# RWKV products over four quarters of TensorE's array, with plain transposes between two layouts

## The chip, the core and the metric

The kernel runs on one core of one Trainium2 chip. Its time is device microseconds from start to end of one execution. The core's engines run their own instruction streams and wait for one another by semaphores: PE (TensorE, matrix products), DVE (VectorE), ACT (ScalarE), POOL (GpSimd), and SP, which in this kernel only issues DMAs. The profile keeps PE's weight loads apart from its products as PEld.

## The reference, cut to what matters

Two transformer blocks run one after the other on 256 tokens with 1024 features, in float32. Block 1 is differential attention and a mixture of 16 experts. Block 2 mixes a sparse attention and an RWKV-7 branch and then goes through a mixture of 32 experts. The change touches the RWKV branch alone, which has 8 heads of 64 features and is a recurrence over tokens:

```python
def step(state, inp):
    r_t, d_t, k_t, v_t, kk_t, b_t = inp
    sa = jnp.einsum('bhij,bhj->bhi', state, -kk_t)
    state = state * d_t[:, :, None, :] + sa[..., None] * b_t[:, :, None, :] + v_t[..., None] * k_t[:, :, None, :]
    y = jnp.einsum('bhij,bhj->bhi', state, r_t)
    return state, y
```

The experts' weights are 6 MB for each expert in either block and are read once.

## The kernel before

**Layout of the RWKV branch.** The 256 tokens are cut into 4 chunks of 64. Two heads lie on the two halves of the 128 partitions, so four pairs of heads times four chunks make 16 places, and a tile of 16 x 64 columns holds one 64 x 64 matrix for each of 8 heads and 4 chunks. `H2` is the pair of partition halves, `r_` one of them. Every product in `products` and `chunk_chain` is 64 x 64 by 64 x 64 (or 64 x 128), and it reads and writes the same half: `T.matmul(ps[r_, i], a[r_, i], b[r_, i])`. Two such products, one for each half, thus stand on two of the four quarters of the array, the ones on its diagonal.

**`products`** makes the triangular matrix of each chunk (`prod`, line 1646), masks it (line 1650) and inverts it in five levels (lines 1702 to 1732): `abT` by `X` (line 1707), a mask on DVE (line 1710), `Pm` by `XT` (line 1717), a subtraction on DVE (line 1721), and `XT` turned into the next `X` by products with the identity (line 1727) and a copy on ACT (line 1730). The generator `side` holds work that the levels do not need yet: `tokens` turns four tensors from features on partitions to tokens on partitions, by products with the identity too (line 1659), and a second `prod`. `take(side, 2)` inserts two of its steps at a time. **`chunk_chain`** applies the inverse (line 1753), makes the operators of a chunk (lines 1765 to 1774), their sums `N` (lines 1781 to 1785), two links of the recurrence (line 1792) and the output (lines 1803 to 1809). Everything takes its PSUM banks from one ring of four, `pr`.

**Order of the work.** There is no planner of times: `weave` draws steps from generators, always from the one whose summed yields are lowest, and while these run it hands steps of a `fill` generator in between. Of each positive yield a share of 0.4 is credit for the fill, and a step of the fill (`fm3g`, three products of 128 x 128 by 256 columns, lines 684 to 686) costs 0.33. The order so drawn is the order of instructions on each engine. Block 2 weaves four generators with this fill:

```python
weave((ds.topk(), 0.5),
      (chain(ds.qkv(x), ds.heads(lambda: bank(c))), 1.0),
      (conditions(), 0.8),
      (rwkv(), 1.0), fill=fill(), ratio=0.4, waits=0.1)
```

The fill holds the gates of both branches and the projection of the attention branch; what is left of it when the generators end is run behind them. `conditions` multiplies modulation weights on DVE (lines 460 to 463), and the weights of each projection are split into two parts by ACT and DVE (lines 628 and 629).

**SBUF units and the stream of weights.** SBUF is handed out in `NU` units of 8 KB per partition (1 MB each). `Stream` holds some of them as slots; it loads weights in a fixed order on SP's queue, and each load waits until its slot's last reader is done. Ahead of the experts of block 2 the stream takes 14 units (`st.size(14)`, line 2193), and `st.grow()` (lines 2220 and 2225) adds what is free. Each expert takes six loads of 1 MB.

Of the kernel before, what the change touches and what calls it, by code (L numbers as in the profile page):

```python
# [16 lines left out]
P = 128  # L17
# [5 lines left out]
NU = 21  # L23
# [1467 lines left out]

class Rwkv:
# [131 lines left out]
    def products(self, pb):  # L1624

        c, sl = self.c, self.sl
# [3 lines left out]
        abT, X, XT, Pm = (sl.get(64) for _ in range(4))  # L1630
# [22 lines left out]
        def tokens(src, dst, cp):  # L1653
# [23 lines left out]

        def others():
            yield from tokens(chunks(self.bt), bb[:, :, 0], A.copy)
            sl.free(self.bt)  # L1680
            vt, ktt = self.vt, self.ktt = chunks(self.v), chunks(self.kt)
            yield from tokens(vt, vt, A.copy)
            self.akT, self.bkT = sl.get(64), sl.get(64)
            yield from prod(self.kt, self.akT, self.bkT)
            yield from tokens(ktt, ktt, A.copy)
            self.uR = c.un.raw()
            self.R = two(self.uR)
            yield from tokens(kkr[:, :, 0], self.R[:, :, 1], A.copy)

            for o in os:  # L1690
# [7 lines left out]
                yield 1.1 / 2  # L1698
            sl.free(self.akT)
        side = others()  # L1700

        for l in range(1, 6):
            for o in os:
                ps = half()
                for i in range(8):
                    for r_ in H2:
                        T.matmul(ps[r_, i], abT[r_, o.start + i], X[r_, o.start + i], start=True, stop=True)
                    if i == 3:
                        yield 1.1 / 2
                V.tensor_tensor(Pm[:, o], ps, bc(c.lev[:, l], 8), ALU.mult)  # L1710
                yield 1.1 / 2
                yield from take(side, 2)
# [10 lines left out]
            for o in os if l < 5 else ():  # L1723
                px = half()
                for i in range(8):
                    for r_ in H2:
                        T.matmul(px[r_, i], XT[r_, o.start + i], c.ident[r_, r_], start=True, stop=True)
                    if i == 3:
                        yield 1.1 / 2
                A.copy(X[:, o], px)  # L1730
                yield 1.1 / 2
                yield from take(side, 2)
        yield from side
        sl.free(abT, X, Pm)

    def chunk_chain(self, pb):
# [23 lines left out]
        for hp in range(4):  # L1760
            ps = quarter()
            for ci in range(4):
                i = 4 * hp + ci
                for r_ in H2:
                    T.matmul(fl(ps[r_, ci]), UG[r_, i, 1], fl(bb[r_, i]), start=True, stop=True)
                if ci == 1:
                    yield 0.9 / 2
# [8 lines left out]
        for o in os:  # L1776
            ps = half()
            for i in range(8):
# [4 lines left out]
                if i == 3:  # L1783
                    yield 3.0 / 2
# [13 lines left out]
        for o in os:  # L1798
            ps = half()
            for i in range(8):  # L1800
# [6 lines left out]
                if i == 3:  # L1807
                    yield 3.9 / 2
# [605 lines left out]
```

## Time and profile before

| | us |
|---|---|
| median of 3 runs | 1343.98 (1343.59 to 1347.93) |
| the profiled execution, its own time | 1341.36 |
| its span, first to last instruction | 1339.8 |

| engine | busy us | share of the span |
|---|---|---|
| PE | 1146.8 | 86% |
| PEld | 705.4 | 53% |
| DVE | 592.5 | 44% |
| ACT | 347.0 | 26% |
| POOL | 101.7 | 8% |

The span is 1.6 us shorter than the execution's own time; a sum of changes inside the span carries over to that time. The shares are means over stages with different limits and have to be read by stage. A product of float32 matrices that is not a transpose is recorded as two instructions, so 320 recorded ones on line 1707 are 160 products.

### The profile page before, as it was taken

To read this page: it belongs to the slowest core of one execution; us is meant where nothing else is said; L and a number is where in the kernel's file an instruction comes from. 1 tells how busy PE (TensorE), PEld (TensorE's weight loads), DVE (VectorE), ACT (ScalarE), POOL (GpSimd) and SP (SyncE) were. 2 spreads that over 40 slices of the span, in tenths; PEclk is the share of its full clock that TensorE was granted. 3 is DMA by queue.
4 is the path that set the end of the run, shared out by engine and by line. 5 is a ranking of instruction groups with operands and counts; after the bars stand their busy time and mean duration, and the time that the engine had idled before them with its cause. 6 is when DMAs were issued, how large, how long until landed. Compare 5 with 4: busy or idle time off the path is not lost. (4 is left out here: it accounts for less than half of the span.)

```text
span 1339.8 us, 20574 instructions
## 1 busy us (share of the span) xinstructions
PE 1146.8 (86%) x8434; PEld 705.4 (53%) x8434; DVE 592.5 (44%) x1464; ACT 347.0 (26%) x675; POOL 101.7 (8%) x111
## 2 busy tenths in 40 slices
PE   5899977899998986988999999889876797677775
PEld 2777767444434335876788888844332242233221
DVE  4477653333225137698555747343222222222212
ACT  3335331211111124552232224232111111111111
POOL 2421110000001003002410010000000000000000
PEclk7999978899999996999999999989889988999898
DMA  8777756699996953350135628769999999999996
GB/s 302 288 276 267 277 223 274 282 418 419 420 384 246 418 218 123 127 187 34 64 140 208 205 94 331 281 256 417 420 419 420 419 420 420 419 420 418 421 419 267
DMA packets 60516, 404.09 MB, mean 302 GB/s; under 512 B 7328, under 2 KB 7584, under 8 KB 14464
## 3 DMA queue, kind: packets, MB, share of 16 engines
q1 hardware_dynamic: 58464, 400.58, 74.6%
q10 hardware_dynamic: 1824, 2.00, 0.5%
q8 instruction: 68, 1.11, 0.3%
q0 software_dynamic: 128, 0.13, 0.2%
q14 instruction: 32, 0.26, 0.1%
HBM read 401.64 MB, written 1.05 MB: 301 GB/s over the span
## 5 line engine op out<-in xcount | busy, mean ns | idle before, releaser
L1218 PE MATMUL a<-u,u 128*32 128x512 f32 (+1 forms) x1536 | 297.8, 614 | 36.2 <-DMA u<-in_expert_w_up 25.3
L1198 DVE SCALAR_TENSOR_TENSOR gs<-a,gc,gt 128x512 f32<-128x512 f32 (+1 forms) x50 | 37.5, 750 | 367.5 <-PE a L1227 360.2
L1227 PE MATMUL a<-u,hid 128*32 128x512 f32 (+1 forms) x736 | 135.5, 623 | 40.7 <-DMA u<-in_expert_w_down 40.7
L1218 PEld LDWEIGHTS a<-u,u 128*32 128x32 f32 (+1 forms) x1536 | 71.1, 119 | 176.6 <-issue 106.9
L684 PE MATMUL a<-u,u 128*128 128x256 f32 x656 | 141.5, 292 | 1.9 <-DVE u L629 1.9
L684 PE MATMUL a<-u,hi 128*128 128x256 f32 x640 | 136.5, 304 | 0.4 <-ACT u L1531 0.4
L1156 ACT COPY gs<-a 128x512 f32<-128x512 f32 x48 | 28.1, 586 | 335.8 <-PE a L1218 326.1
L684 PEld LDWEIGHTS a<-u,u 128*128 128x128 f32 x656 | 104.4, 193 | 12.7 <-issue 9.2
L684 PEld LDWEIGHTS a<-u,hi 128*128 128x128 f32 x640 | 99.3, 191 | 15.6 <-issue 8.9
L1200 ACT CAST u<-gs 64x512 fp32r<-64x512 f32 x96 | 59.2, 616 | 183.3 <-DVE gs L1198 182.2
L1227 PEld LDWEIGHTS a<-u,hid 128*32 128x32 f32 (+1 forms) x736 | 33.3, 119 | 124.2 <-DMA u<-in_expert_w_down 52.1
L1202 DVE TENSOR_TENSOR u<-gs,u 64x512 fp32r<-64x512 f32 x96 | 65.9, 686 | 27.2 <-ACT u L1200 25.3
L628 ACT CAST hi<-u 128x1024 fp32r<-128x1024 f32 x48 | 49.8, 1047 | 72.0 <-PE a L684 60.0
L629 DVE TENSOR_TENSOR u<-u,hi 128x1024 fp32r<-128x1024 f32 x48 | 61.7, 1291 | 14.7 <-ACT hi L628 14.2
L908 PE MATMUL a<-u,u 128*128 128x256 f32 x256 | 49.0, 312 | 9.2 <-DVE u L629 8.0
L629 POOL TENSOR_TENSOR u<-u,u 128x512 fp32r<-128x512 f32 (+1 forms) x22 | 44.5, 2041 | 127.2 <-ACT u L628 127.2
L1163 PEld LDWEIGHTS a<-sel,gs 128*128 128x128 f32 x256 | 35.1, 212 | 28.4 <-issue 26.3
L1254 PE MATMUL acc<-u,PT 128*128 128x512 f32 x128 | 44.4, 460 | 5.2 <-DVE u L1202 3.6
L1140 PE MATMUL a<-pm,u 128*128 128x256 f32 x256 | 40.8, 315 | 8.1 <-DVE gs L1198 3.2
L908 PEld LDWEIGHTS a<-u,u 128*128 128x128 f32 x256 | 40.4, 216 | 10.3 <-DVE u L629 8.2
L1254 PEld LDWEIGHTS acc<-u,PT 128*128 128x128 f32 x128 | 22.3, 208 | 44.1 <-DVE u L1202 34.3
L763 PE MATMUL e<-u,u 128*128 128x256 f32 x288 | 40.1, 306 | 5.5 <-ACT u L591 5.0
(447 smaller groups left out, 1599.9 us busy)
## 6 DMA issues: line engine op xcount, KB each, us to landing
u<-in_expert_w_gate SPq DMA_DIRECT2D x96, 1024.0 KB, 19.9
u<-in_expert_w_up SPq DMA_DIRECT2D x96, 1024.0 KB, 19.9
u<-in_expert_w_down SPq DMA_DIRECT2D x96, 1024.0 KB, 19.9
u<-in_ada_w SPq DMA_DIRECT2D x32, 1024.0 KB, 6.9
u<-in_w_in SPq DMA_DIRECT2D x19, 1024.0 KB, 4.9
u<-in_ada_w SPq DMA_DIRECT2D x32, 512.0 KB, 3.9
u<-in_attn_w_in SPq DMA_DIRECT2D x12, 512.0 KB, 7.8
u<-in_attn_w_in SPq DMA_DIRECT2D x6, 1024.0 KB, 7.4
```

The lines of the kernel that those rows point to most:

```text
L628: nc.scalar.copy(h[:, o], w[:, o])
L629: (nc.vector if e == "v" else nc.gpsimd).tensor_tensor(l[:, o], w[:, o], h[:, o].bitcast(F32), ALU.subtract)
L684: c.nc.tensor.matmul(ps, a[:, k, c0:c0 + n], b[:, k], start=k == 0 and i == 0, stop=k == kn - 1 and i == 2)
L763: T.matmul(p[:, j * S:(j + 1) * S], l, r, start=(h, j, k, n) == (0, 0, 0, 0), stop=(h, k, n) == (1, 3, 2), skip_group_check=True)
L908: self.c.nc.tensor.matmul(ps[:, j * S:(j + 1) * S], a[:, k, j * P:(j + 1) * P], b[:, k], start=k + j + i == 0, stop=k == KD - 1 and i == 2 ...
L1140: nc.tensor.matmul(ps[:, jj * m:(jj + 1) * m], h[:, t, k * P:(k + 1) * P], pm[:, t], start=i + jj + t == 0, stop=i + t == 2, skip_group_ch ...
L1198: c.nc.vector.scalar_tensor_tensor(out=y[o], in0=py[o], scalar=gc[o], in1=gt[o], op0=ALU.mult, op1=ALU.mult)
L1200: c.nc.scalar.copy(yy[H2[q], q], y[H2[q]])
L1202: c.nc.vector.tensor_tensor(yy[H2[1 - q], q], y[H2[q]], yy[H2[q], q].bitcast(F32), ALU.subtract)
L1218: c.nc.tensor.matmul(pg[r:r + cap], xe[:, k0 + k, x0:x0 + cap], w[:, k, :], start=k0 + k < nk, stop=k0 + k >= KD - nk)
L1227: c.nc.tensor.matmul(py[r:r + cap], hT[:, f], w[:, f - f0, q * 512:(q + 1) * 512], start=f < nk, stop=f >= 4 - nk)
L1254: c.nc.tensor.matmul(acc[:, 2 * t + q], PT[:, t * P:(t + 1) * P], yy[:, q], start=False, stop=stop, skip_group_check=True)
```

## The change

All quarters of the array get work. A second layout puts the tokens of a chunk on the half of the chunk's parity (even chunks on partitions 0 to 63, odd ones on 64 to 127), and features stay on the half of the head. A product that contracts over features and writes tokens (or the other way) then reads one half and writes either, and four products that follow each other, `quads(y)`, stand on four different quarters. This holds for `prod`, the first product of a level, the operators, the sums and most of the output; products from tokens to tokens stay on two quarters. The two row halves of a group of four write to two different PSUM banks. Going from one layout to the other is now a plain transpose of 128 x 128 (`turned`), where it was a product with a 64 x 64 identity. The first product of a level needs `abX`, the matrix in the other layout, which is made by 32 more products and two copies on ACT. The terms of the recurrence's output that come from the chunk before get a PSUM bank of their own and are added on DVE. A copy of `kkr` on ACT goes ahead of one turn. Yields and the numbers of side steps taken change with the steps. `NU` goes from 21 to 22, and the kernel is built with a smaller scratch area for dynamic DMAs.

```diff
-NU = 21
+NU = 22
...
+def quads(y):
+    return [(2 * y + c, h, 2 * y + h) for c in range(2) for h in range(2)]
...
         def prod(src, o1, o2):
             lhs = chunks(src)
-            for hp in range(4):
-                ps = pb()
-                p4 = ps.rearrange("p (c a s) -> p c a s", c=4, a=2)
-                for ci in range(4):
-                    i = 4 * hp + ci
-                    for r_ in H2:
-                        T.matmul(fl(p4[r_, ci]), lhs[r_, i], fl(kkr[r_, i]), start=True, stop=True)
-                    if ci == 1:
-                        yield 0.9 / 2
-                for o, a in ((o1, 0), (o2, 1)):
-                    V.tensor_tensor(o[:, 4 * hp:4 * hp + 4], p4[:, :, a], bc(c.mlt[:, a], 4), ALU.mult)
-                yield 0.9 / 2
...
+            for x in (0, 8):
+                ps = [pb().rearrange("p (c a s) -> p c a s", c=4, a=2) for _ in H2]
+                for y in range(4):
+                    for i, h, j in quads(x // 2 + y):
+                        T.matmul(fl(ps[h][H2[i % 2], y]), lhs[H2[h], i], fl(kkr[H2[h], i]), start=True, stop=True)
+                    yield 0.3
+                for h in range(2):
+                    for o, a in ((o1, 0), (o2, 1)):
+                        V.tensor_tensor(o[:, x + h:x + 8:2], ps[h][:, :, a], bc(c.mlt[:, a], 4), ALU.mult)
+
+        def turned(src, dst, cp):
             for o in os:
                 ps = half()
-                for i in range(8):
-                    for r_ in H2:
-                        T.matmul(ps[r_, i], src[r_, o.start + i], c.ident[r_, r_], start=True, stop=True)
-                    if i == 3:
-                        yield 1.1 / 2
+                for i in range(0, 8, 2):
+                    T.transpose(fl(ps[:, i:i + 2]), src[:, o.start + i:o.start + i + 2], c.ident)
+                    if i % 4:
+                        yield 0.3
                 cp(dst[:, o], ps)
-                yield 1.1 / 2
...
+        for o in os:
+            ps = half()
+            for i in range(8):
+                for r_ in H2:
+                    T.matmul(ps[r_, i], chunks(self.bt)[r_, o.start + i], kkr[r_, o.start + i, 0], start=True, stop=True)
+                if i == 3:
+                    yield 1.1 / 2
+            A.copy(abX[:, o], ps)
+            yield 1.1 / 2
+        sl.free(abT)
...
         for l in range(1, 6):
-            for o in os:
-                ps = half()
-                for i in range(8):
-                    for r_ in H2:
-                        T.matmul(ps[r_, i], abT[r_, o.start + i], X[r_, o.start + i], start=True, stop=True)
-                    if i == 3:
-                        yield 1.1 / 2
-                V.tensor_tensor(Pm[:, o], ps, bc(c.lev[:, l], 8), ALU.mult)
-                yield 1.1 / 2
-                yield from take(side, 2)
+            ps = half(), half()
+            for y in range(8):
+                for i, h, j in quads(y):
+                    T.matmul(ps[h][H2[i % 2], y], abX[H2[h], i], X[H2[h], i], start=True, stop=True)
+                if y % 2:
+                    yield 0.35
+            for h in range(2):
+                V.tensor_tensor(Pm[:, h::2], ps[h], bc(c.lev[:, l], 8), ALU.mult)
+            yield from take(side, 4)
...
+            if l < 5:
+                for _ in turned(XT, X, A.copy):
+                    yield 0.3
+                    yield from take(side, 1)
...
+        def two_sums(pairs):
+            ps = half(), half()
+            for z, (a, b) in enumerate(pairs):
+                for y in range(8):
+                    for i, h, j in quads(y):
+                        T.matmul(ps[i % 2][H2[h], y], a[H2[i % 2], j], b[H2[i % 2], j], start=z + y == 0, stop=z == 1,
+                                 skip_group_check=True)
+                    if y % 2:
+                        yield 0.4
+            return ps
+        ps = yield from two_sums([(ktt, vt), (bb[:, :, 0], UG[:, :, 0])])
+        for a in range(2):
+            A.copy(N[:, a::2], ps[a])
...
+        ps = yield from two_sums([(vt, self.bkT), (UG[:, :, 0], bb[:, :, 1])])
+        for a in range(2):
+            V.tensor_copy(yc[:, a::2], ps[a])
         for o in os:
             ps = half()
             for i in range(8):
-                k = o.start + i
-                for r_ in H2:
-                    T.matmul(ps[r_, i], vt[r_, k], self.bkT[r_, k], start=True, stop=False)
-                    T.matmul(ps[r_, i], UG[r_, k, 0], bb[r_, k, 1], start=False, stop=k % 4 == 0)
-                    if k % 4:
-                        T.matmul(ps[r_, i], N[r_, k - 1], MQ[r_, k, 1], start=False, stop=True)
-                if i == 3:
-                    yield 3.9 / 2
-            V.tensor_copy(yc[:, o], ps)
-            yield 3.9 / 2
+                for r_ in H2 if i % 4 else ():
+                    T.matmul(ps[r_, i], N[r_, o.start + i - 1], MQ[r_, o.start + i, 1], start=True, stop=True)
+                if i % 4 == 3:
+                    yield 0.4
+            for x in (1, 5):
+                y3 = yc[:, o.start + x:o.start + x + 3]
+                V.tensor_tensor(y3, y3, ps[:, x:x + 3], ALU.add)
...
-    nc = bacc.Bacc("TRN2", target_bir_lowering=False, num_devices=1)
+    nc = bacc.Bacc("TRN2", target_bir_lowering=False, num_devices=1, dynamic_dma_scratch_size=4096)
```

The operators (line 1765 before) change in the same way as `prod`, with a yield of 0.3 after each group of four.

## Rows read from the trace of the kernel before

**Rows 1.** Four stretches: window, length, busy us (instructions) by engine, clock, DMA.
```profile
630.00:833.00 203.00, 201.33 (x2646) 166.17 (x2646) 122.66 (x234) 60.19 (x111) 26.99 (x28) 1.00 0.47 172
833.00:867.00 34.00, 32.06 (x272) 31.75 (x272) 14.02 (x22) 9.31 (x16) 0.23 (x4) 1.00 0.71 280
867.00:883.00 16.00, 7.85 (x42) 7.36 (x42) 11.43 (x55) 4.62 (x10) 0.00 (x0) 0.68 0.19 67
883.00:1323.30 440.30, 347.14 (x2168) 136.01 (x2168) 111.06 (x267) 73.16 (x138) 0.00 (x0) 0.95 1.01 418
```

**Rows 2.** Chain that ended last, two of its pieces: start, us, what.
```profile
893.62 12.74 DMA u<-in_expert_w_up
...
1302.90 20.41 DMA u<-in_expert_w_down
```

**Rows 3.** Timeline of SP's queue at 848 to 883: start, us, issue, tensor.
```profile
848.19 0.33 SPq L128 DMA_DIRECT2D u<-in_expert_w_up  x1
862.16 5.20 SPq L128 DMA_DIRECT2D u<-in_expert_w_down  x2
882.07 0.33 SPq L128 DMA_DIRECT2D u<-in_expert_w_gate  x1
```

**Rows 4.** Timeline of PE in levels 4 and 5 and the chunks.
```profile
742.63 0.68 PE L1707 MATMUL b<-u,u 64*64 64x64 f32 x16
743.24 0.51 PE L684 MATMUL a<-u,hi 128*128 128x256 f32 x2
743.59 0.28 PE L684 MATMUL a<-u,u 128*128 128x256 f32 x1
743.80 0.68 PE L1707 MATMUL b<-u,u 64*64 64x64 f32 x16
...
755.30 1.15 PE L1707 MATMUL b<-u,u 64*64 64x64 f32 x32
...
764.26 1.96 PE L1753 MATMUL b<-u,u 64*64 64x128 f32 x32
```

**Rows 5.** Groups by line and shape, 630 to 833: count, busy us, mean ns, idle.
```profile
L462 DVE SCALAR_TENSOR_TENSOR mvsum<-u,cond_c,mvsum 128x512 f32<-128x512 f32 x49 | 36.6, 748 | 2.4 <-DMA u<-in_ada_w 1.8
L629 DVE TENSOR_TENSOR u<-u,hi 128x1024 fp32r<-128x1024 f32 x23 | 28.3, 1239 | 5.8 <-ACT hi L628 5.6
L1707 PE MATMUL b<-u,u 64*64 64x64 f32 x320 | 13.6, 223 | 0.0
L1727 PE MATMUL b<-ident,u 64*64 64x64 f32 x256 | 10.7, 223 | 0.0
L1646 PE MATMUL b<-u,u 64*64 64x128 f32 x128 | 10.2, 279 | 0.0
L1710 DVE TENSOR_TENSOR u<-b,u 128x512 f32<-128x512 f32 x10 | 6.9, 689 | 5.6 <-PE b L1707 5.6
L1804 PE MATMUL b<-u,u 64*64 64x64 f32 x64 | 5.5, 218 | 0.0
```

**Rows 6.** Timeline of PE, three steps of line 684 without a break.
```profile
820.27 0.40 PE L684 MATMUL a<-u,hi 128*128 128x256 f32 x2
820.51 0.29 PE L684 MATMUL a<-u,u 128*128 128x256 f32 x1
820.64 0.39 PE L684 MATMUL a<-u,hi 128*128 128x256 f32 x2
```

**Rows 7.** Timeline of PE: plain transposes (line 836), then the next product.
```profile
98.77 0.60 PE L836 MATMUL a<-ident,sc 128*128 128x128 f32 x4
99.12 0.36 PE L684 MATMUL a<-u,u 128*128 128x256 f32 x1
```

**Rows 8.** Timeline of PE: products of 256 columns on parts of the array.
```profile
89.47 0.70 PE L811 MATMUL s<-u,u 64*128 64x256 f32 x4
...
808.67 0.64 PE L702 MATMUL a<-u,hs 128*32 128x256 f32 x8
...
813.82 1.99 PE L1842 MATMUL a<-grows,u 128*128 128x256 f32 x8 [0.50 <-ACT grows L726]
```

More of the change, by code (lines that the diff above doesn't have):

```diff
@@ L1629, in products @@
         two = lambda t: t.rearrange("p (i a s) -> p i a s", i=16, a=2)
-        abT, X, XT, Pm = (sl.get(64) for _ in range(4))
+        abT, abX, X, XT, Pm = (sl.get(64) for _ in range(5))
         self.ubb = c.un.raw()
@@ L1676, in products @@
             yield 1.1 / 2
+        for o in os:
[8 more added lines that the diff above has]
+        sl.free(abT)
         def others():
[L1679 removed]
+            yield from turned(chunks(self.bt), bb[:, :, 0], A.copy)
             sl.free(self.bt)
             vt, ktt = self.vt, self.ktt = chunks(self.v), chunks(self.kt)
[L1682 removed]
+            yield from turned(vt, vt, A.copy)
             self.akT, self.bkT = sl.get(64), sl.get(64)
             yield from prod(self.kt, self.akT, self.bkT)
[L1685 removed]
+            yield from turned(ktt, ktt, A.copy)
             self.uR = c.un.raw()
             self.R = two(self.uR)
[L1688 removed]
             for o in os:
@@ L1698, in others @@
                 yield 1.1 / 2
+            A.copy(self.akT, kkr[:, :, 0])
+            yield from turned(self.akT, self.R[:, :, 1], A.copy)
             sl.free(self.akT)
@@ L1722, in products @@
                 yield from take(side, 2)
-            for o in os if l < 5 else ():
-                px = half()
-                for i in range(8):
-                    for r_ in H2:
-                        T.matmul(px[r_, i], XT[r_, o.start + i], c.ident[r_, r_], start=True, stop=True)
-                    if i == 3:
[L1729 to L1732, printed above, removed]
+            if l < 5:
+                for _ in turned(XT, X, A.copy):
+                    yield 0.3
+                    yield from take(side, 1)
         yield from side
-        sl.free(abT, X, Pm)
+        sl.free(abX, X, Pm)
     def chunk_chain(self, pb):
@@ L1759, in chunk_chain @@
         N = sl.get(64)
[L1760 to L1767, printed above, removed]
-            o = slice(4 * hp, 4 * hp + 4)
-            V.tensor_tensor(MQ[:, o, 0], ps[:, :, 0], c.eye.unsqueeze(1).to_broadcast([P, 4, 64]), ALU.add)
-            V.tensor_tensor(MQ[:, o, 1], ps[:, :, 1], kkr[:, o, 1], ALU.add)
-            o1 = slice(4 * hp + 1, 4 * hp + 4)
-            G.tensor_tensor(MQ[:, o1], MQ[:, o1],
-                            self.dec[:, 4 * hp:4 * hp + 3].unsqueeze(2).unsqueeze(3).to_broadcast([P, 3, 2, 64]), ALU.mult)
-            yield 0.9 / 2
@@ L1776, in chunk_chain @@
-        for o in os:
-            ps = half()
-            for i in range(8):
-                k = o.start + i
-                for r_ in H2:
-                    T.matmul(ps[r_, i], ktt[r_, k], vt[r_, k], start=True, stop=False)
-                    T.matmul(ps[r_, i], bb[r_, k, 0], UG[r_, k, 0], start=False, stop=True)
-                if i == 3:
-                    yield 3.0 / 2
-            A.copy(N[:, o], ps)
-            yield 3.0 / 2
+        for x in (0, 8):
+            ps = quarter(), quarter()
+            for y in range(4):
+                for i, h, j in quads(x // 2 + y):
+                    r_ = H2[i % 2]
+                    T.matmul(fl(ps[i % 2][H2[h], y]), UG[r_, j, 1], fl(bb[r_, j]), start=True, stop=True)
+                yield 0.3
+            for a in range(2):
+                o = slice(x + a, x + 8, 2)
+                V.tensor_tensor(MQ[:, o, 0], ps[a][:, :, 0], c.eye.unsqueeze(1).to_broadcast([P, 4, 64]), ALU.add)
+                V.tensor_tensor(MQ[:, o, 1], ps[a][:, :, 1], kkr[:, o, 1], ALU.add)
+            for i in (x, x + 4):
+                G.tensor_tensor(MQ[:, i + 1:i + 4], MQ[:, i + 1:i + 4],
+                                self.dec[:, i:i + 3].unsqueeze(2).unsqueeze(3).to_broadcast([P, 3, 2, 64]), ALU.mult)
@@ L1797, in chunk_chain @@
         yc = chunks(yT)
+        ps = yield from two_sums([(vt, self.bkT), (UG[:, :, 0], bb[:, :, 1])])
+        for a in range(2):
+            V.tensor_copy(yc[:, a::2], ps[a])
         for o in os:
```

4 lines of the change are left out of this document (removed).

## The prediction, made before the changed kernel ran

> **What bounds the kernel now.** I read the table of stretches first, because the shares of the whole span mix stages. From 630 to 833 us, where the RWKV products lie, PE is busy for 201.33 of 203.00 us at a granted clock of 1.00, while DVE is busy for 122.66 and the DMA engines for 0.47 of the time; so PE's queue alone sets this stretch [rows 1]. From 833 to 867 PE is still full with the last projections, and from 867 to 883 the router's chain of small steps runs and the DMA engines are nearly idle at 0.19. From 883 to 1323.3 the DMA engines are full at 418 GB/s, and PE is busy for only 347 of 440 us [rows 1]. Then I read the chain of waits: from 893.62 on it is loads of expert weights, until the last one that starts at 1302.90; 16.5 us of last products and stores follow [rows 2]. The experts of block 2 are 192 loads of 1 MB. Up to 867 SP issues 16 of them; the 17th has to wait until 882.07 [rows 3]. The remaining 176 take 440 us, 2.5 us each, and this fits 1.05 MB at 418 GB/s.
>
> So what PE saves between 630 and 833 moves all that follows, the full stretch of loads included, and comes off the end one to one. A load more that is in SBUF before 882 takes 2.5 us off.
>
> **What a product costs.** In a run of 32 recorded instructions on line 1707, the run lasts 1.15 us and one instruction 0.22, so they start (1.15 - 0.22) / 31 = 0.030 us apart: 0.060 for a pair on the two diagonal quarters. With 128 columns it is (1.96 - 0.28) / 31 = 0.054, or 0.108 for a pair [rows 4, 5]. Changing between products of 64 x 64 and of 128 x 128 costs extra. Sixteen instructions of line 1707 hold PE from 742.63 to 743.24, 0.61 where 16 x 0.030 = 0.48 would do. Three of line 684 hold it from 743.24 to 743.80, 0.56 [rows 4], and without a break from 820.27 to 820.64, 0.37 [rows 6]. So one visit to the small shape costs 0.13 + 0.19 = 0.32 us beside its products.
>
> **The change part by part.**
>
> (a) Groups of four. By 128 columns: 128 recorded on line 1646 and 64 on line 1765. By 64 columns: 320 on line 1707, and 64 each on lines 1781, 1782, 1803 and 1804, of which one row stands [rows 5]. They now take 192 x 0.054 + 576 x 0.030 = 10.4 + 17.3 = 27.7 us. If four run in the time of two, half of it goes: -13.8. No row shows four quarters at once. But eight products on column quarters with all rows take 0.64 us, where eight of the same 256 columns on the whole array take 1.99 less 0.50 that may lie between; and four products on two row halves, each writing all output partitions to its own bank, take 0.70 [rows 8]. Both ways of sharing work by themselves, so I take the whole half. The bounds are 0 (the second column half waits, as slow as now) and -13.8.
>
> The Trainium skill speaks against it: "TensorE: Matmul & The Clock Gate", section "Wait — 56ns, not 53.3ns?", says that starts come no closer than about 25 ns however few columns there are. The rows' mean of 30 ns between starts does not contradict it. By it a group of four by 64 columns takes 100 ns and not 60, the part by 64 columns shrinks to 576 x (30 - 25) ns = 2.9 us, and the sum would come out at 1322.
>
> (b) Turns. 256 recorded products on line 1727 and as many on line 1659 take 512 x 0.030 = 15.4 us [rows 5]. In their place stand eight turns (four in the levels, four beside them) of eight plain transposes. Four transposes and the step to the next product take from 98.77 to 99.12, and four from first to last start plus one duration 0.60 [rows 7]; I take 0.11 each: 64 x 0.11 = 7.0. That is -8.4. The bound on the other side is the whole 0.60 for four, 0.15 each: -5.8.
>
> (c) `abX`: 64 more recorded products, 64 x 0.030 = +1.9, and two copies on ACT that hide, because ACT is busy for 60 of 203 us [rows 1]; the same holds for the copy of `kkr`.
>
> (d) Visits to the small shape. Before there are 124 yielded steps of small products, 96 in `products` and 28 in `chunk_chain`. In the timeline a step mostly stands alone between two fill steps, as at 742.63, or with one neighbour, as at 755.30 [rows 4]; I estimate 0.8 visits per step, 100 in all. After there are 106 such steps, since the turns leave the small shape; and 72 of them yield 0.3 to 0.45, so a fill step (0.33, from 0.4 of the yields) falls behind every second or third one and not behind two of three. With 0.6 for these and 0.8 for the 32 steps of 0.55, and some five visits that a turn between small products adds, I get about 75. That is -25 x 0.32 = -8.0; bounds 10 and 45 visits, -3 and -14. The fill's steps that are no longer drawn in between run behind the generators, at 0.37 each, as PE's total asks.
>
> (e) The unit. It is free when `st.grow()` runs, so a 17th load goes out while the DMA engines idle: -2.5. Bounds 0 and -2.5. In block 1, where no wait of PE ends on a load, I give it nothing. The smaller scratch concerns a few small POOL DMAs at the start; I take 0, and the sum has no term for it.
>
> (f) New waits. PE is idle for under 2 us of the stretch now [rows 1], because the two halves of a level cover each other: while one is masked, the other multiplies. After the change both masks (0.69 each [rows 5]) come behind the last of the eight groups, and the next product needs both. In levels 1 to 3 four side steps of some 0.9 us stand between, and I leave 0.5 us open; in levels 4 and 5 the side work is used up and about 1.4 us stay open: 3 x 0.5 + 2 x 1.4 = 4.3. The two copies of `N` now end together, +0.6. DVE's queue holds 49 multiplications of 0.75 us and 23 splits of 1.24 us [rows 5], and now and then one will lie ahead of a mask: +1. Together +6, with bounds 0 and +20. The four small additions at the end of the output replace the later half of a copy, and I give them nothing.
>
> The sum: -13.8 - 8.4 + 1.9 - 8.0 - 2.5 + 6 = -24.8. From the profiled execution's 1341.36 that gives 1316.6, and I say 1317. The runs' median stands 2.6 us above that execution, so a median might stand at 1319; the range covers it.
>
> **The rivals.**
>
> *Four quarters are no faster than two.* PE gets a pair's two starts together and then the next pair 0.060 later; no row shows a denser stream of products by 64 columns for longer than a few instructions. If the pace of 0.030 per instruction is that of issuing or of loading weights, and not of the array, the part by 64 columns gains nothing (8.6 less) and the part by 128 still gains: 1325. If two column halves of one row half never overlap, all of (a) is gone: 1330. For it: no row has both ways of sharing at once. Against it: by 128 columns PE takes 0.054 per instruction, so issuing is not what spaces those.
>
> *The waits take it all (the other side).* The products use banks from a ring of four, and after the change they take two at a time. By the code some 66 banks are taken, and each is free again only when DVE or ACT has read it; DVE's queue is in order and holds the pieces of 0.75 and 1.24 us. Without (f) the gain is 30.8 us, so 0.47 us of PE's waiting per bank eats it, and from there the kernel is slower; at 0.6 it would be 1350. For it: DVE is busy for 60% of the stretch [rows 1], and would be for about 70% of a shorter one. Against it: ahead of 10 masks DVE stood idle for 5.6 us in all, waiting for PE [rows 5], so its queue is mostly ahead.
>
> *More than forecast.* If the side and fill steps cover the masks and clusters of visits merge further, (f) goes to 0 and (d) to -14: 1305.
>
> **How the numbers follow.** I give the forecast 0.58, its own range being 1308 to 1325; the first rival 0.20 (1322 to 1331); more than forecast 0.10 (1302 to 1308); the waits 0.12, of which 0.02 still ends faster, 0.05 near no change, and 0.05 slower. A measurement here tells a difference from none at about 0.3%, 4 us. Faster: 0.58 + 0.20 + 0.10 + 0.02 = 0.90; same 0.05; slower 0.05. The range leaves out the worst of the waits and the best of the gain: 1304, which is all the gains at their bounds, to 1334, which is (a) at nothing (1330), the runs' median 2.6 above the profile, and a little more waiting.
>
> **What would show it.** In the profile after, a run of line 1707's successor should have four starts in the time of two: 16 recorded in about 0.4 us and not 0.68; the turns should be x64 with 128 x 128 at 0.11 us; steps of line 684 should more often stand in longer runs. The router's idle stretch should begin at about 845 and not at 867, and SP should issue 17 expert loads ahead of it. The full stretch of loads should last 437 us. The prediction is wrong if PE's idle time between 630 and 833 grows from 2 us to more than 15, if groups of four start no closer than 0.030 us on the mean, or if the end moves less than the start of the full stretch of loads.

## The result and the profile after

The changed kernel takes 1321.26 us in the median of 4 runs (1320.02 to 1322.14), beside 1345.32 for the kernel before (4 runs, 1343.59 to 1347.93): a ratio of 0.9823 with a 95% interval of 0.9803 to 0.9844. Timed again beside the experiments it is 0.9841 (0.9803 to 0.9878). The forecast was 1317, range 1304 to 1334, faster.

The profiled execution takes 1321.29 us, span 1319.7: 20.1 less than the profiled one before. The stretches after, to be held against [rows 1]; the columns are the same, and the stretches hold the same pieces of work:

```profile
632.00:815.00 183.00, 177.48 (x2273) 144.55 (x2272) 127.16 (x242) 63.17 (x117) 26.44 (x28) 1.00 0.54 197
815.00:849.00 34.00, 32.23 (x272) 31.92 (x272) 13.81 (x23) 9.12 (x16) 0.23 (x4) 1.00 0.75 279
849.00:865.00 16.00, 8.41 (x42) 7.92 (x42) 11.43 (x54) 4.27 (x9) 0.00 (x0) 0.68 0.19 67
865.00:1303.00 438.00, 346.35 (x2168) 137.52 (x2168) 111.29 (x268) 73.71 (x138) 0.00 (x0) 0.95 1.01 418
```

From the first product of `prod` to the first of `wob` it is 183.1 us, where it was 203.1. PE is busy for 177.48 of 183.00, so it now waits for 5.5 us, where it waited for some 2. What follows comes some 18 us earlier, because the stage itself begins 1.8 us later (632.0 and not 630.3): the router's idle stretch begins at 849 and not at 867, the experts at 865.7 and not at 883.2, and the loads run at the same 418 GB/s. From the first product of `wob` to the end it is 504.6 us, where it was 506.5. So the profile's 20.1 us are 20.0 of the stage, less 1.8 lost ahead of it, plus 1.9 behind it. It is still PE's queue that sets this stage, and loads that set the rest.

Groups of lines from 632 to 815, to be held against [rows 5] (1722 is the successor of 1707, 1664 of 1727 and 1659, 1653 of 1646, 1726 of 1710):

```profile
L462 DVE SCALAR_TENSOR_TENSOR mvsum<-u,cond_c,mvsum 128x512 f32<-128x512 f32 x49 | 37.8, 772 | 10.8 <-DMA u<-in_ada_w 10.2
L629 DVE TENSOR_TENSOR u<-u,hi 128x1024 fp32r<-128x1024 f32 x24 | 29.1, 1222 | 6.7 <-ACT hi L628 6.6
L1664 PE MATMUL b<-ident,u 128*128 128x128 f32 x64 | 11.3, 276 | 0.0
L1722 PE MATMUL b<-u,u 64*64 64x64 f32 x320 | 8.2, 227 | 0.0
L1653 PE MATMUL b<-u,u 64*64 64x128 f32 x128 | 7.1, 288 | 0.0
L1726 DVE TENSOR_TENSOR u<-b,u 128x512 f32<-128x512 f32 x10 | 6.5, 682 | 0.1
L2028 PE MATMUL a<-ident,u 128*128 128x128 f32 x24 | 4.5, 282 | 2.0 <-POOL u L2021 2.0
L1834 PE MATMUL a<-u,u 128*128 128x512 f32 x4 | 2.1, 611 | 1.1 <-DVE u L1822 1.1
L1804 PE MATMUL b<-u,u 64*64 64x64 f32 x32 | 1.4, 224 | 1.3 <-DVE u L1805 1.3
```

One instruction of line 1722 lasts 227 ns, one of line 1707 lasted 223; only more of them overlap. No line of the levels has any waiting. What waits is the recurrence (1804), the normalisation behind it (1834) and the attention's heads (2028). The timeline of PE, against [rows 4]:

```profile
686.90 0.69 PE L1722 MATMUL b<-u,u 64*64 64x64 f32 x32
689.34 0.46 PE L1722 MATMUL b<-u,u 64*64 64x64 f32 x16
...
697.48 0.38 PE L1664 MATMUL b<-ident,u 128*128 128x128 f32 x2
...
747.69 0.89 PE L1774 MATMUL b<-u,u 64*64 64x128 f32 x24
```

Sixteen take 0.46 us where they took 0.68, and 32 take 0.69 where they took 1.15. The single records of the run at 686.90 start 7, 6 and 7 ns apart, and then 38 ns pass (87 behind the first four): four recorded instructions start every 58 ns. In the run of line 1707 at 755.30 it is 7 and 52 ns: two every 59 ns. As each product is recorded as two instructions, four products on four quarters take two such steps, some 116 ns. SP's queue, against [rows 3]:

```profile
848.94 0.33 SPq L128 DMA_DIRECT2D u<-in_expert_w_gate  x1
864.55 0.33 SPq L128 DMA_DIRECT2D u<-in_expert_w_up  x1
867.65 0.33 SPq L128 DMA_DIRECT2D u<-in_expert_w_gate  x1
```

The 17th load goes out at 848.94, while the DMA engines idle, and not when the stage of the experts begins.

**Where PE's time went.** I add up, for each PE instruction of the stage, the time from its start to the next one's start, less any waiting. Products of 64 x 64: 77.1 us before, 47.2 after. The 64 transposes: 0 and 6.8. Line 684: 89.9 and 87.0. The rest: 34.1 and 36.5; 2.8 us more of it are work of the attention's heads that ran ahead of the stage before. Waiting: 2.0 and 5.6. Together 203.1 and 183.1.

### The profile page after: what moved, and what is told of

It reads as the page before. It is cut to its first block, busy times and chain, and to the rows that moved or that the text cites. A ratio compares the mean times of both kernels' runs of the same rounds, so it can differ in the third digit from the quotient of the medians.

```text
span 1319.7 us, 19811 instructions
## 1 busy us (share of the span) xinstructions
PE 1129.5 (86%) x8050; PEld 691.6 (52%) x8050; DVE 598.3 (45%) x1468; ACT 348.1 (26%) x678; POOL 101.1 (8%) x111
## 5 line engine op out<-in xcount | busy, mean ns | idle before, releaser
L1218 PE MATMUL a<-u,u 128*32 128x512 f32 (+1 forms) x1536 | 293.8, 608 | 32.8 <-DMA u<-in_expert_w_up 23.1
L684 PE MATMUL a<-u,u 128*128 128x256 f32 x656 | 142.9, 295 | 2.6 <-DVE u L629 2.6
L684 PEld LDWEIGHTS a<-u,u 128*128 128x128 f32 x656 | 106.2, 196 | 12.6 <-issue 9.2
L1200 ACT CAST u<-gs 64x512 fp32r<-64x512 f32 x96 | 59.2, 616 | 193.1 <-DVE gs L1198 191.9
L629 DVE TENSOR_TENSOR u<-u,hi 128x1024 fp32r<-128x1024 f32 x48 | 63.7, 1333 | 15.4 <-ACT hi L628 15.1
L908 PE MATMUL a<-u,u 128*128 128x256 f32 x256 | 51.5, 325 | 6.1 <-DVE u L629 5.3
L1185 DVE CAST PT<-a 128x256 fp32r<-128x256 f32 x48 | 20.4, 425 | 67.4 <-PE a L1183 34.0
L1163 PEld LDWEIGHTS a<-sel,gs 128*128 128x128 f32 x256 | 35.9, 217 | 28.7 <-issue 25.7
L462 DVE SCALAR_TENSOR_TENSOR mvsum<-u,cond_c,mvsum 128x512 f32<-128x512 f32 x56 | 43.1, 769 | 11.6 <-DMA u<-in_ada_w 10.9
L1140 PEld LDWEIGHTS a<-pm,u 128*128 128x128 f32 x256 | 39.0, 230 | 15.9 <-DVE gs L1198 5.8
```

The source lines that it names most:

```text
L462: V.scalar_tensor_tensor(out=mine[0], in0=w[:, k], scalar=cs[:, k:k + 1], in1=mine[0], op0=ALU.mult, op1=ALU.add)
L629: (nc.vector if e == "v" else nc.gpsimd).tensor_tensor(l[:, o], w[:, o], h[:, o].bitcast(F32), ALU.subtract)
L684: c.nc.tensor.matmul(ps, a[:, k, c0:c0 + n], b[:, k], start=k == 0 and i == 0, stop=k == kn - 1 and i == 2)
L908: self.c.nc.tensor.matmul(ps[:, j * S:(j + 1) * S], a[:, k, j * P:(j + 1) * P], b[:, k], start=k + j + i == 0, stop=k == KD - 1 and i == 2 ...
L1140: nc.tensor.matmul(ps[:, jj * m:(jj + 1) * m], h[:, t, k * P:(k + 1) * P], pm[:, t], start=i + jj + t == 0, stop=i + t == 2, skip_group_ch ...
L1200: c.nc.scalar.copy(yy[H2[q], q], y[H2[q]])
```

## The experiments

Each kernel was timed beside the kernel before on its chip. In the table "stage" is the time from the first product of `prod` to the first of `wob` in the traced execution; "waits" is PE's waiting in it; "half" is the time in it at a granted clock of 0.5 (1.2 and not 2.4 GHz), summed over windows of 0.5 us; "visits" is how often PE goes from other work into products of 64 x 64. One execution of each kernel is traced, and it can lie 5 us from the median (with longer runs 1317.12, median 1322.05; with two column halves 1332.81, median 1328.56).

| kernel | ratio (95%) | stage | waits | half | visits |
|---|---|---|---|---|---|
| before | 1 | 203.1 | 2.0 | 0 | 99 |
| unit alone | 1.0036 (1.0020 to 1.0052) | 205.6 | 2.0 | 0 | 100 |
| the change | 0.9823 (0.9803 to 0.9844) | 183.1 | 5.6 | 0 | 79 |
| the change again | 0.9841 (0.9803 to 0.9878) | 181.9 | 4.6 | 0 | 79 |
| with 21 units | 0.9876 (0.9841 to 0.9911) | 186.6 | 6.5 | 13.7 | 76 |
| two row halves | 0.9905 (0.9873 to 0.9937) | 193.2 | 2.2 | 10.2 | 79 |
| two column halves | 0.9885 (0.9862 to 0.9907) | 191.9 | 2.2 | 6.8 | 77 |
| turns as products | 0.9916 (0.9888 to 0.9945) | 192.1 | 6.5 | 6.8 | 92 |
| before, longer runs | 0.9935 (0.9914 to 0.9956) | 195.4 | 5.8 | 3.4 | 57 |
| longer runs | 0.9836 (0.9805 to 0.9867) | 183.2 | 8.3 | 17.1 | 57 |
| longer runs, later sums | 0.9854 (0.9826 to 0.9882) | 186.9 | 12.2 | 20.5 | 52 |
| later sums alone | 0.9864 (0.9841 to 0.9886) | 190.6 | 10.2 | 10.2 | 74 |
| longer runs, later sums, 21 units | 0.9861 (0.9837 to 0.9885) | 187.2 | 16.6 | 10.2 | 51 |
| longer runs, splits on POOL | 0.9860 (0.9836 to 0.9884) | 184.0 | 12.4 | 13.7 | 52 |

The first theory was the prediction's: four quarters at the price of two, turns at a third of their price, fewer visits, a small loss by waits, and a load more ahead of the experts.

### The unit, taken back and taken alone

```diff
-NU = 22
+NU = 21
...
-    nc = bacc.Bacc("TRN2", target_bir_lowering=False, num_devices=1, dynamic_dma_scratch_size=4096)
+    nc = bacc.Bacc("TRN2", target_bir_lowering=False, num_devices=1)
```

> The changed kernel with 21 units and the former scratch area. If the unit is worth the one load that it lets go out ahead of the experts, and no more, this takes 2.5 us longer than the changed kernel: about 1324. The rival: the unit also changes the order of instructions ahead of the products, where the changed kernel's profile stands about 5 us behind the kernel before at 631 us (it stood 0.8 behind at 499). Then taking it away gives those 4 to 5 us back and the sum is about 1319. SP should issue 16 expert loads ahead of the stage and not 17 in either case.

The other kernel is before with the opposite edit.

> The kernel before with 22 units and the smaller scratch area, nothing else. By the one load: about 1342.8, 2.5 us faster than before. By the rival, that the unit's new order ahead of the products costs some 4 to 5 us: 1345 to 1348, no faster than before. The products themselves should be untouched: 32 recorded instructions of line 1707 in 1.15 us.

The unit alone makes the kernel 0.36% slower, 4.8 us. In the stream of loads it does what was forecast: from the first load issued behind their first product to the last one it takes 419.4 us, and 422.7 before. In all the traces of this study it is 419.3 to 420.3 with 22 units (ten traces) and 422.0 to 422.7 with 21 (four). But ahead of `wob` it costs 4.5 us: from block 2's first projection to the first product of `wob` 329.0 us pass, and 324.5 before. SP's queue in the kernel with the unit alone, and then in the kernel before:

```profile
564.27 24.95 SPq L128 DMA_DIRECT2D u<-in_w_in  x4
601.15 15.08 SPq L128 DMA_DIRECT2D u<-in_ada_w  x6
```

```profile
564.29 13.00 SPq L128 DMA_DIRECT2D u<-in_w_in  x3
582.71 0.80 SPq L128 DMA_DIRECT2D u<-in_ada_w  x2
588.91 0.33 SPq L128 DMA_DIRECT2D u<-in_w_in  x1
591.80 8.49 SPq L128 DMA_DIRECT2D u<-in_ada_w  x4
```

With 22 units the conditions' weights are issued 18 us later, and PE's wait at line 724, some 20 us ahead of the stage, is 4.75 us instead of 2.72. That this delay is the whole cost was not tested, and two things speak against putting it down to the unit as such. Two kernels further down with 21 units ("before, longer runs" and "longer runs, later sums, 21 units") issue these weights at 602 and 601 us too and wait 4.70 and 4.75 us there. And from block 2's first projection to the stage 28.7 us run at half clock with the unit alone and 18.0 before; it is 18.0 as well in the change with 21 units, which issues the weights early, and 27 us or more in all the others. Nor do 3.3 us won and 4.5 lost add up to the 5.7 by which the two traces differ. From the first product of `wob` to the end the trace with the unit alone takes 508.5 us, 2.0 more than the one before, in spite of its shorter stream; this stretch varies from 503.9 to 508.8 us with 22 units and from 506.5 to 510.0 with 21. So the 4.8 us are shown as the price of this build, and only in part explained.

Taking the unit back out of the change gives 0.9876, no better than with it; but its trace has 13.7 us at half clock in the stage that the change's two traces do not have, so this pair decides nothing. The pair further down, 1326.19 with the unit and 1326.06 without, shows no difference either way, but both of these issue the conditions' weights late.

### Two quarters at a time

```diff
-                for y in range(4):
-                    for i, h, j in quads(x // 2 + y):
-                        T.matmul(fl(ps[h][H2[i % 2], y]), lhs[H2[h], i], fl(kkr[H2[h], i]), start=True, stop=True)
-                    yield 0.3
+                for n, (y, i, h, j) in enumerate(twos(range(x // 2, x // 2 + 4), True)):
+                    T.matmul(fl(ps[h][H2[i % 2], y - x // 2]), lhs[H2[h], i], fl(kkr[H2[h], i]), start=True, stop=True)
+                    if n % 4 == 3:
+                        yield 0.3
```

`twos` gives the same products in an order in which only the two row halves of one column half meet; the three other places of `quads` change alike. A second kernel lets only the two column halves of one row half meet.

> The changed kernel with the same products in another order: all that use one column half of the array first, then the other, so that two row halves run side by side and never four quarters. Counts, yields, banks and turns are unchanged. If the gain of the groups of four is that four run in the time of two, 13.8 us come back, less what lies in the shadow of other work: 1331 to 1336, and 16 recorded instructions of the first product of a level take 0.68 us where they take 0.46. If the groups of four gained nothing and the turns and the fewer visits did it all, it stays at 1321.

> The changed kernel with the same products in an order in which only the two column halves of one row half meet, and never four quarters. With two row halves at a time the same lines took 0.0385 to 0.041 us per recorded instruction of 64 columns, against 0.022 in groups of four and 0.038 on the diagonal before. If column halves overlap as row halves do, this is the same: some 0.040 on the first product of a level (7.1 us become 13), and the stage grows by about 8 to 10 us to 192, ratio about 0.990. Rival (the prediction's lower bound): column halves of one row half never overlap, each instruction then takes twice as long, 0.060 to 0.080, the first product of a level takes 20 to 25 us and the stage 200 to 215, ratio about 1.00. Other rival: column halves are as good as four, because loading weights into one half beside a running other half is all that is gained; then the lines take 0.022 and the stage stays at 183.

The timeline of PE with two row halves, and then with two column halves:

```profile
726.88 1.44 PE L1728 MATMUL b<-u,u 64*64 64x64 f32 x48
...
728.57 0.68 PE L1728 MATMUL b<-u,u 64*64 64x64 f32 x16
```

```profile
727.44 1.44 PE L1728 MATMUL b<-u,u 64*64 64x64 f32 x48
```

Both ways of pairing cost the same as the diagonal pairs of before: starts 7 and 52 ns apart, 59 ns for two recorded instructions. All products of 64 x 64 together take 58.6 and 57.8 us and not 47.2, some of it in the half-clock stretches of their traces, and 0.4 to 0.8 points of per cent of the change's gain are gone. So one round over the quarters costs 58 or 59 ns, whether two of them or four are in it.

### Turns as products, in groups of four

```diff
-            for o in os:
-                ps = half()
-                for i in range(0, 8, 2):
-                    T.transpose(fl(ps[:, i:i + 2]), src[:, o.start + i:o.start + i + 2], c.ident)
-                    if i % 4:
-                        yield 0.3
-                cp(dst[:, o], ps)
+            ps = half(), half()
+            for y in range(8):
+                for i, h, j in quads(y):
+                    T.matmul(ps[h][H2[i % 2], y], src[H2[h], i], c.ident[H2[h], H2[h]], start=True, stop=True)
...
```

The masks of `prod` also go ahead of its last yield here.

> The changed kernel with the turns made by products with a 64 x 64 identity, as before, but in groups of four; masks of the first products come before their last yield and not behind it, for the banks' sake. If what made the turns cheap is the plain transpose as such (64 recorded products of 0.030 us against 8 transposes of 0.11), 8.4 us come back: about 1330. If groups of four would have done the same (64 x 0.015 = 0.96 us a turn against 0.87), only 0.7 us of products and about 10 more visits to the small shape at 0.32 us come on top: about 1325.

The turns' 512 recorded products take 11.4 us, the 64 transposes 6.8, the visits rise from 79 to 92, and the ratio is 0.9916. By the trace the transposes with the visits that they spare are worth 9 us of the stage less what 6.8 us at half clock took, some 3.4: about 5.6 us. By the medians it is 0.8 to 0.9 points of per cent, 10 to 12 us, more than either alternative had; the traced execution (1326.78) was the fastest of six. The masks that were moved are part of this run, and their share was not tried by itself.

### Fewer and longer runs of small products

```diff
-            credit += y * ratio if y > 0 else -y * waits
-            while credit > 0:
-                y = next(fill, None)
+            credit, low = credit + (y * ratio if y > 0 else -y * waits), lump
+            while credit > low:
+                y, low = next(fill, None), 0.0
```

With `lump=0.66` in block 2's `weave`, on the change and on the kernel before. The change itself ran again beside them.

> The changed kernel once more, timed beside the next three on one chip, as their measure. In its first trace the granted clock is 1.00 in every 8 us stretch from 620 us to the end of the chains. In the traces of the last group of experiments it fell to 0.50 for some microseconds inside this stage: 14 us in the one with 21 units, 10 us with two rows halves at a time, 7 us with turns as products. Theory A: the fall belongs to how these kernels order PE's work, the changed kernel has none, the stage from the first product to the first branch_out of `wob` is 183 us again, and the ratio to before is 0.982. Rival B: the fall comes in some executions of any kernel of this family in which the light parts of the queue meet a short wait; then the changed kernel shows it too in some executions, its runs spread by up to 7 us as those of the kernel with 21 units did (1319 to 1330), and the profiles of one execution each can't be compared to a few microseconds without taking the half-clock stretches out.

> The kernel before with the same edit alone: 57 entries into small products instead of 99, all else as before, diagonal pairs and turns as products. Theory: 42 fewer at 0.32 us give 13.4 us, the stage of 203 us becomes about 190 and the time about 1331, half of the change's gain without touching the layout. Rival: entries are not what costs, or the two halves of a level no longer cover each other's masks when less stands between them; then PE's idle time grows from 1.6 us to 10 and more and the time stays near 1343.

> The changed kernel, with one edit in the loop that mixes the branches' products in: they are drawn only when 0.66 us are due, and then until nothing is due, so that fewer and longer runs of them stand between the small products. PE's order has 57 entries into small products instead of 79. Theory: an entry costs 0.32 us (0.13 on the small side and 0.19 on the large one, from the rows of before), so 22 fewer give 7.0 us: the stage 183 becomes 176 and the time about 1312 to 1314. Rival: the entry costs nothing by itself, it is only PE's waiting for its operands that shows there, or the longer runs of small products leave masks uncovered; then PE's idle time grows from 5.3 us by as much as is saved, and the time stays within 3 us of the changed kernel's or is worse.

On the kernel before, 42 visits fewer take line 684 from 89.9 to 78.6 us and the small products from 77.1 to 71.3, 0.41 us for a visit; I had put it at 0.32. The Trainium skill ("TensorEngine Tiling (Array Packing)", section "Key Properties") says that a change of tiling mode drains the engine; it gives no price. The 0.41 us is what a visit cost here, there and back; that draining is what takes the time, no run here shows. The time falls by 0.65%, 8.7 us, and not by 13.4: PE's waits grow from 2.0 to 5.8 us, 3.4 us run at half clock, and its order, like that with 22 units, has 2.8 us of the heads' work behind the first product.

On the change the same edit gives nothing: 0.9836 beside 0.9841. Line 684 falls from 86.8 to 80.8 us, but the waits rise by 3.7, and 17.1 us of the stage run at half clock. The clock in three windows of it, and PE's timeline at the place where it falls:

```profile
720.00:728.00 8.00, 6.30 (x124) 5.53 (x122) 4.36 (x7) 2.02 (x3) 0.00 (x0) 0.96 0.60 223
728.00:736.00 8.00, 8.00 (x100) 6.98 (x101) 3.55 (x6) 1.14 (x2) 0.00 (x0) 0.50 0.18 63
736.00:744.00 8.00, 8.00 (x119) 7.05 (x119) 6.54 (x10) 3.50 (x6) 0.00 (x0) 0.90 0.55 185
```

```profile
724.59 0.69 PE L1722 MATMUL b<-u,u 64*64 64x64 f32 x32
726.98 1.07 PE L487 MATMUL a<-ones,mvsum 128*128 128x1 f32 x6 [1.70 <-DVE mvsum L462]
727.99 1.13 PE L1722 MATMUL b<-u,u 64*64 64x64 f32 x32
```

PE waits 1.70 us for the conditions' multiplication on DVE, then does six recorded products of a single column; the run of 32 behind it takes 1.13 us where the one ahead took 0.69. In the kernel with 21 units it is the same line, 0.81 us of waiting at line 487, and then:

```profile
740.00:743.00 3.00, 2.35 (x45) 1.68 (x34) 2.96 (x6) 0.00 (x0) 1.65 (x2) 1.00 0.00 0
743.00:753.00 10.00, 9.85 (x136) 8.48 (x137) 7.59 (x13) 1.83 (x3) 2.57 (x3) 0.53 0.50 159
```

### The row sums later, and DVE relieved

So I made a second theory: what PE waits for at line 487 lets the clock fall, and without these waits the longer runs pay. `matvecs` gets a wait of 5.0 units instead of 3.0, so that line 487 is drawn later; with longer runs, without them, and with 21 units.

```diff
-            ... "vvvvvvvv", 0.5, 3.0, rows, "0123")
+            ... "vvvvvvvv", 0.5, 5.0, rows, "0123")
```

> The kernel with fewer, longer runs, and in block 2 the conditions' row sums (products of 128 x 1 on line 487) drawn 2 units later behind the multiplications they wait for. In the kernel with longer runs alone PE waited 3.8 of its 8.0 us of idle time at line 487 for the multiplication of line 462, and the clock fell to half right behind such places, at 727.3 behind 1.70 us of waiting and at 751.3 behind 2.07 us, 17 us at half in the stage in all, which cost 8.5. Theory: thin work (one column per product, small products, a wait) is what lets the clock fall, so with the wait at line 487 gone the idle time falls to about 4 us, the time at half clock to 7 us or less, the stage from 183 to about 173 to 176, and the time to about 1310, ratio 0.975. Rival: the clock falls because fewer visits leave longer runs of small products, waits or not; then 10 us and more stay at half clock, the stage stays above 178, and the ratio stays at 0.983.

> The changed kernel with the conditions' row sums drawn later, and nothing else. The changed kernel has 0.7 us of waiting at line 487 and, in its two traces, no fall of the clock in the stage; its timed executions spread over 14 us on the second chip (1315 to 1330). If falls behind line 487 happen in some of its executions, as the trace of the kernel with 21 units suggests (0.81 us of waiting there at 743.15, then 10 us at half), the spread shrinks and the median falls by 2 to 4 us to about 1317, ratio 0.981. Rival: the spread comes from elsewhere (ahead of this stage or in the loads), the median stays within 2 us and the spread as it is.

> The same as the kernel with longer runs and later row sums, but with 21 units and the program's usual scratch. With 22 units the stream of waiting loads lasted 419 to 420 us in five traces, with 21 it lasted 422 to 423 in three, so the unit gives 2.5 us there; ahead of it the traces of 22 units have 2 us more in the stretch before the products and 2.8 us of work (lines of the token mixing's heads) that 21 units have ahead of the stage. If the second outweighs the first, as the run of the unit alone says (4.8 us slower than before), this kernel is 2 to 4 us faster than the one with 22 units, ratio about 0.973. Rival: the unit pays in this order of work, and this kernel is 2 us slower.

The theory falls. With longer runs and later sums no wait at line 487 is left, but others took its place, and 20.5 us run at half clock; groups of PE in the stage:

```profile
L684 PE MATMUL a<-u,u 128*128 128x256 f32 x193 | 57.6, 299 | 4.5 <-DVE u L629 4.5
L2028 PE MATMUL a<-ident,u 128*128 128x128 f32 x24 | 4.7, 303 | 2.9 <-POOL u L2021 2.7 <-ACT u L2122 0.2
L498 PE MATMUL a<-mvsum,ones 128*64 128x512 f32 x4 | 3.0, 846 | 1.6 <-DVE mvsum L462 1.6
```

Later sums alone cost the change 3 to 5.5 us by the medians (0.9864 against 0.9823 and 0.9841; the intervals overlap); their executions spread over 7 us where the change's spread over 14 in its second timing. The last trial asks whether DVE's queue is what holds PE: the second half of 12 splits goes to POOL.

```diff
-    c.sp = Splits(c, [(n, "vv") for n in PLAN.split()], [hi1])
+    c.sp = Splits(c, [(n, "vg" if n[0] == "g" or n[:2] == "wb" else "vv") for n in PLAN.split()], [hi1])
```

> The kernel with fewer, longer runs (the row sums as in the changed kernel), and the second half of each split of the gates' and branches' weights on POOL instead of DVE: 12 of the 24 subtractions of 1.22 us that DVE has in the stage (line 629) leave it, 14.6 us of its 131; POOL, busy for 28 of 183 us, takes some 2.5 us for each, from its 1.28 us for 128 x 512, and has room. PE's order has 52 entries into small products. In the kernel with later row sums the waits only moved: 3.8 us at line 487 went, and 4.5 us at line 684 for DVE's line 629, 1.6 at line 498 and others came, and 20 us at half clock stood in the stage. Theory: what takes back the saved visits is DVE's queue, which holds the multiplications, splits and masks that PE waits for, and the clock follows the waits; then PE's idle time falls from 8 to about 5 us, the time at half clock from 17 us to 7 or less, the stage from 183 to about 175, the ratio to about 0.977. Rival: shorter work on PE alone, between the same chains of steps, leaves it idle and at half clock whichever engine holds the steps; POOL's slower half now comes late for line 684; then idle and half clock stay at 8 and 14 us or more and the ratio at 0.983 to 0.986.

The rival holds. DVE is busy for 125 us and POOL for 54, and line 684 has no waits, yet PE waits 12.4 us, half of it for the small steps of the chain itself:

```profile
L1732 PE MATMUL b<-u 64*64 64x64 f32 x320 | 12.1, 222 | 1.7 <-DVE u L1726 1.7
L1762 PE MATMUL b<-u,u 64*64 64x128 f32 x64 | 3.9, 272 | 1.6 <-DVE u L1736 1.6
L1804 PE MATMUL b<-u,u 64*64 64x64 f32 x32 | 1.4, 224 | 2.8 <-DVE u L1805 2.8
```

Line 684 is down to 79.8 us here (so the rival's remark that POOL's half comes late for it was wrong), but the stage is at 184.0, and ahead of it 6.6 us more pass from block 2's first projection to the first product (130.0 where the change has 123.4). None of these versions beats the change.

## Why the prediction was right, and where its terms were off

**Groups of four (a).** Forecast -13.8 of 27.7 us. The lines concerned take 34.2 us before and 20.6 after (1722, 1653, 1774, 1791), the small side of the visits included: -13.6. The halving was right (two starts every 59 ns became four every 58, and by 128 columns two every 109 became four every 109), and the two kernels with pairs show that it needs all four quarters: row halves alone or column halves alone bring nothing over the diagonal. The first rival fell, and with it the rule of the Trainium skill that was weighed there ("TensorE: Matmul & The Clock Gate", "Wait — 56ns, not 53.3ns?"): starts on different quarters come 6 to 7 ns apart, and the mean in a run is 15 ns, where the rule has 25. The second rival, waits, took 3.6 us and not 31.

**Turns (b) and visits (d).** Forecast -8.4 and -8.0. The turns fell from 19.0 us (1727 and 1659) to 6.8, -12.1 (0.107 each, 0.11 forecast): I had priced the old ones at 0.030 an instruction, without the visits that stood among them, which I had put under (d). What (d) has left is 3.0 us on line 684, where 20 visits fewer at 0.27 us each (11.3 us for 42, in before with longer runs) would give 5.4; where the difference went is not shown. The visits are 79 and not 75. Both terms together: -15.1, forecast -16.4.

**`abX` (c).** 2.45 us, forecast 1.9.

**New waits (f).** Forecast +6, measured +3.6, but at other places. I had them at the levels' masks; there line 1722's successors have none. Two masks of 0.68 us come behind the first product of each level, and what lies between covers them, in levels 4 and 5 too. The waits came in the recurrence, behind the output and at the heads, where the work that hid them had shrunk.

**The unit (e).** Forecast -2.5 at the loads, and the stream of loads shows 3.3 with the unit alone and 2.6 in the change. The step that failed is "Bounds 0 and -2.5": they leave out a loss, and the build with the unit alone has one, 4.5 us ahead of `wob` in the traces and 4.8 us in the time. Without it the forecast's terms for the stage sum to -22.3; from the unit alone (205.6 us, same heads inside) to the change the stage falls by 22.5. The profiles differ by 20.1 us and the medians by 24.1; the forecast was 24.8. It was taken off 1341.36, an execution 4 us below the median of 1345.32. Between the profiles it was 4.7 us too much, between the medians 0.7; that it fits the medians so closely is in part luck, since the unit's 2.5 us were not gained in the whole.

**A correction.** The text ahead of the prediction says that the order drawn is the order on each engine. That is too strong: the kernel holds single instructions to their place with `keep_in_program_order`, and others may be moved when the program is built; with the unit alone the order on PE differs from block 1 on, though no step was changed. My count of visits from yields came out near (79 for 75) all the same.

**What stays open.** The executions of the change spread over 14 us in its second timing (1315 to 1330), and only one there is traced. The mean granted clock is on record for each: 0.948 and 0.949 in the executions of 1315 and 1316 us, 0.934 in those of 1327 and 1330. So the longer ones had more half-clock time; whether it lay in this stage is not shown. Nor is it settled what makes the clock fall in one order of PE's work and not in another. In the traces it fell behind waits and behind thin products at line 487, but with two row halves also where the one wait near was 0.13 us, with later sums in the middle of a wait of 2.5 to 7.1 us, and in three places where no wait above 0.1 us stands in the 8 us ahead (659.1 with longer runs, 694.8 with longer runs and later sums, 664.6 with splits on POOL); and taking the waits at line 487 away did not remove it.

## What to carry to other kernels

When products of 64 x 64 stand on a diagonal, a second layout that gives the other two quarters work halves the time between their starts, and a plain 128 x 128 transpose is a cheap way between the layouts. Count the changes of shape on PE as work: at 0.41 us each, 99 of them were, by estimate, 40 us of this stage. But once a stage has so little work left that its chains show, PE's savings go into waits and half-clock stretches: here four versions that take 3 to 7 us more off line 684 left the time where it was or made it worse.

## What the runs showed of the hardware that I had not expected

Recorded products by 64 columns start two every 59 ns on any two quarters, on the diagonal, in one column half or in one row half, and four every 58 on four: the spacing goes with the return to the same quarter. By 128 columns it is 109 ns for two and for four, so it grows with the columns. And the granted clock fell to 0.5 inside a stage in which PE was busy for 95% of the time (174.9 of 183.2 us with longer runs, for 3.4 and 10.2 us at once); in the change's two traces it did not.
